# One stream of key tiles through a three-mixer attention kernel, with maxima and sums taken apart between two engines

## The chip, the cores and the metric

One core of a Trainium2 chip runs the whole program. The metric is device time in microseconds (us), and less is better. Five engines take part: TensorE (PE, with its weight loads shown as PEld), VectorE (DVE), ScalarE (ACT), GpSimd (POOL) and SyncE (SP, which issues the DMAs). Each works through its own instructions in order and waits on semaphores for the others.

## The reference

An input of 2048 rows by 1024 columns goes through one encoder layer in float32. After a modulated RMS norm, one projection feeds three groups of attention heads; their gated outputs are projected back, added to the input and normed.

```python
h = rmsnorm(x, norm_g) * (1.0 + scale) + shift
z = h @ w_in
a_out = mla_mixer(...)           # 6 heads, q and k of 64 + 32 rotary columns, mask by chunks of 64
b_out = chunk_band_mixer(...)    # 5 heads, own chunk + 8 chunks before, relative bias
c_out = forgetting_mixer(...)    # 5 heads, causal by frame, forget-gate bias in the logits
y = concat([a_out*silu(a_gate), b_out*silu(b_gate), c_out*silu(c_gate)]) @ w_out
out = rmsnorm(x + gate * y, final_g)
```

Each mixer is a softmax over the keys that its mask allows, times the values: `p = softmax(where(mask, s, -1e30)); o = p @ v`.

## The kernel before, in words

The rows are worked off in two halves of 1024. In each half, `stage_lv` makes the latent projections and the values, and `attention` then goes through 16 heads; each head has two blocks of 512 queries. At the end of half 1 comes the output projection (`out_units`), the last half of it after the attention.

Products that need float32 accuracy are split into a high and a low part of type fp32r, so a projection (`mm3_units`, L348 to L350) is three matmuls per 128 rows of contraction, and a score tile is two or three.

A block goes over its key tiles of 128 keys. One tile is `scores(n)`: the matmuls into a PSUM bank `st` (three banks; L994 and L1009 for kinds B and C, L1070, L1071 and L1074 for kind A), three exponentials on ACT (L744, L745, L747: the high part `ph`, a float32 copy `p32`, and one in place), the low part `pl` on DVE (L748), and the running sum `acc` on POOL (L753). Three tiles later `values(n)` multiplies by the values (L762, L763) into the one PSUM bank `pv`. After the last tile, `end()` does the three value products that are left, copies `pv` out on ACT (L775, L777) and adds its halves on POOL (L778).

A block needs the maximum of each query row before its first score. `max_units` forms score rows on PE into one of two PSUM banks `mx` (L968, L979, L1057), DVE reduces each (L971, L980, L1058), and the last unit, `fin`, ends the chain at once: DVE reduces once more (L985, L1062), and in `m_rows` negates (L704), rounds (L705) and subtracts for a low part (L706); PE transposes the 128x128 pad (L708); DVE spreads the result by a mask into rows 96 to 127 of the query tile (L709).

The denominators take three later steps (`tail`): `sums` transposes `acc` on PE (L787), DVE adds up (L788), inverts (L789) and splits (L793, L794); `rows` transposes the 128x32 pad (L800) and masks it into 512 columns (L801); `gate` multiplies by a matrix of ones (L808), so that every partition has every inverse, DVE multiplies by the gate path (L810), POOL by the values (L811), and a DMA stores.

What sets the order: `attention` calls one unit per tile, and after each unit calls shares of two lists: `fill` (projections and loads of the next head, output projection, next half's input) and maxima of the next block. The order in the source is a priority; a scheduler at build time moves instructions within it, and on the chip each engine keeps the resulting order.

```python
def step(n):
    scores(n)
    if n >= LAG:
        values(n - LAG)
```

Of the kernel before, what the change touches and what calls it, by code (L numbers as in the profile page):

```python
# [61 lines left out]
def kernel(ctx: ExitStack, tc: tile.TileContext, a: dict, out: bass.AP):  # L62
# [195 lines left out]
    mall = const.tile([128, 128], BF16, name="mall")  # L258
    V.memset(mall, -BIG)
# [3 lines left out]
    rpads = [const.tile([128, 32], F32R, name=f"rpad{i}") for i in range(2)]  # L263
    rrow = const.tile([128, 512], F32R, name="rrow")
    for t in mpads + rpads + [rrow]:
        G.memset(t.bitcast(F32), 0.0)
# [43 lines left out]
    def gate_row(pool):  # L310
# [11 lines left out]
        for c in range(2):  # L322
            p = pst("pj")
            T.matmul(p, lhsT=ones, rhs=acc[:, 512 * c:512 * c + 512], start=True, stop=True)
            V.tensor_tensor(bg[:, 512 * c:512 * c + 512], p[0:1, :], bg[:, 512 * c:512 * c + 512], op=ALU.add)
        dma(out=d_gate, in_=bg)
# [372 lines left out]
    def m_rows(pool, m4, dst, c8=None):  # L699

        mp = mpads[counters["m"] % 2]
        counters["m"] += 1
# [4 lines left out]
        tp = pst("mx")  # L707
        T.transpose(tp[:, 0:128], mp.bitcast(F32), ident)  # L708
        V.tensor_tensor(dst[96:128, :].rearrange("p (j t) -> p j t", j=4),  # L709
                        tp[96:128, None, 0:128].to_broadcast([32, 4, 128]),  # L710
                        mmask[96:128, :].rearrange("p (j t) -> p j t", j=4), op=ALU.mult)

    def body_units(pool, kind, tb, par, scale, qk, V_of, sg_of, dst):
# [12 lines left out]
        def scores(n):  # L726
# [13 lines left out]
            v0, v1 = c0, c1  # L740
            p32 = pool.tile([128, 512], F32, tag="acc" if n == 0 else "p32", name="p32", bufs=2 if n == 0 else 4)
            ph = pool.tile([128, 512], F32R, tag="ph", name="ph", bufs=PB)
            pl = pool.tile([128, 512], F32R, tag="pl", name="pl", bufs=PB)
# [4 lines left out]
            V.tensor_tensor(pl[:, v0:v1], st[:, v0:v1], ph[:, v0:v1].bitcast(F32), op=ALU.subtract)  # L748
            if n == 0:
                box["acc"] = p32  # L750
            else:
                acc = box["acc"]
                G.tensor_tensor(acc[:, v0:v1], acc[:, v0:v1], p32[:, v0:v1], op=ALU.add)  # L753
            box[n] = (ph, pl, c0, c1)

        def values(n):
# [3 lines left out]
            ph, pl, c0, c1 = box[n]  # L760
# [4 lines left out]
        def step(n):  # L765
            scores(n)
            if n >= LAG:
                values(n - LAG)

        def end():  # L770
            for n in range(max(len(js) - LAG, 0), len(js)):
                values(n)
# [5 lines left out]
            G.tensor_tensor(oa[o0:o1, :], oa[o0:o1, :], ob[o0:o1, :], op=ALU.add)  # L778
            box["oa"] = oa


        def sums():
# [6 lines left out]
            V.reciprocal(s4, s4)  # L789
            i = counters["r"] % 2  # L790
            counters["r"] += 1
            rp = rpads[i]
            V.tensor_scalar(rp[:, 0:4], s4, 0.5, 0.0, op0=ALU.mult, op1=ALU.add)  # L793
            V.scalar_tensor_tensor(rp[:, 4:8], in0=s4, scalar=0.5, in1=rp[:, 0:4].bitcast(F32), op0=ALU.mult, op1=ALU.subtract)  # L794
            box["rp"], box["rw"] = rp, rrow

        def rows():
            rp, rw = box["rp"], box["rw"]
            tp = pst("mx")
            T.transpose(tp[0:32, 0:128], rp.bitcast(F32), ident)  # L800
            V.tensor_tensor(rw[0:32, :].rearrange("p (j t) -> p j t", j=4),  # L801
                            tp[0:32, None, 0:128].to_broadcast([32, 4, 128]),
# [326 lines left out]
    def attention(heads, made, first, mids):  # L1129
# [24 lines left out]
        for _, u in tail:  # L1154
            u()
# [170 lines left out]
```

## Time and profile before

| what | value |
|---|---|
| three runs | 1902.49, 1903.47, 1904.70 us |
| median | 1903.47 us |
| the profiled execution | 1901.45 us |
| its span, first to last instruction | 1899.7 us |
| mean granted TensorE clock, as a share of full speed | 0.971 |
| busy share PE, DVE, ACT, POOL | 92%, 72%, 63%, 53% |

The span is what the profiler records; 1.75 us lie around it. Busy time is the time in which an engine has an instruction in execution. Matmuls overlap, so the start of one to the start of the next says more of PE's pace than the duration of one. An idle time in a group's row is what the engine stood still just before those instructions, and the name behind the arrow is the instruction that ended the wait.

### The profile page before, as it was taken

The numbers are of one execution on the slowest core, as the hardware profiler recorded it, in microseconds if no ns is written. First come the engines' busy times: TensorE is split into PE (matmuls) and PEld (weight loads), VectorE is DVE, ScalarE is ACT, GpSimd is POOL, SyncE is SP. The second block draws the span as 40 slices with busy tenths as digits, with TensorE's granted clock in tenths as the row PEclk, the third lists the DMA queues.
The fourth block names the chain that finished last, engine by engine and source line by source line (L and its number), as shares of the span: only waits on it lengthen the run. The fifth ranks groups of instructions, "written<-read, shape, count | busy, mean of one in ns | idle before, by whom it ended". The sixth has DMA issues, their size and how long they took to land.

```text
span 1899.7 us, 28618 instructions
## 1 busy us (share of the span) xinstructions
PE 1743.7 (92%) x8786; PEld 1416.1 (75%) x8786; DVE 1364.4 (72%) x3204; ACT 1191.9 (63%) x2550; POOL 1009.4 (53%) x943
## 2 busy tenths in 40 slices
PE   3999999898999987899999999999899989898997
PEld 3899877676777764899777787777677667776786
DVE  7764468887868789554567878888788888767543
ACT  2552356576767776342367778889888989554611
POOL 1320145666555656120155656767677878665744
PEclk9999999899999998899999999999999989999999
DMA  7534935334223332133943232222333344232243
GB/s 285 150 96 120 254 113 149 102 110 151 80 77 96 102 99 64 57 120 117 250 116 85 82 89 77 73 57 66 95 98 87 99 121 120 77 100 70 70 136 111
DMA packets 139997, 209.85 MB, mean 110 GB/s; under 512 B 18734, under 2 KB 72494, under 8 KB 139764
## 3 DMA queue, kind: packets, MB, share of 16 engines
q1 hardware_dynamic: 139844, 208.03, 36.7%
q8 instruction: 70, 1.15, 0.2%
q14 instruction: 83, 0.68, 0.1%
HBM read 154.05 MB, written 57.38 MB: 111 GB/s over the span
## 4 chain that ended last, share of the span: by engine, by line
PE 46%; DVE 8%; ACT 3%; issue 2%; POOL 2%; DMA 1%; SPq 0%; POOLq 0%; DVEq 0%; ACTq 0%
PE pj L348 6%; PE pj L350 6%; PE pj L349 6%; PE pv L762 3%; PE pv L763 3%; PE st L1009 2%; PE st L994 2%; PE mx L1057 2%; PE st L1074 2%; PE st L1070 2%; PE mx L968 1%; PE st L1071 1%; DVE pl L748 1%; PE st L348 1%; PE st L349 1%
## 5 line engine op out<-in xcount | busy, mean ns | idle before, releaser
L753 POOL TENSOR_TENSOR p<-p,p 128x512 f32<-128x512 f32 (+2 forms) x516 | 561.5, 1088 | 252.0 <-ACT p L745 194.3
L744 ACT ACTIVATE ph<-st 128x512 fp32r<-128x512 f32 (+1 forms) x580 | 323.1, 557 | 191.5 <-PE pv L762 99.8
L748 DVE TENSOR_TENSOR pl<-st,ph 128x512 fp32r<-128x512 f32 (+1 forms) x580 | 342.5, 593 | 92.8 <-ACT st L747 85.5
L747 ACT ACTIVATE st<-st 128x512 f32<-128x512 f32 (+1 forms) x580 | 330.5, 570 | 0.0
L745 ACT ACTIVATE p<-st 128x512 f32<-128x512 f32 (+1 forms) x580 | 322.9, 557 | 0.9 <-POOL p L753 0.9
L348 PE MATMUL pj<-hT,whi 128*128 128x512 f32 x544 | 223.8, 411 | 8.2 <-ACT q L925 8.2
L349 PE MATMUL pj<-hT,whi 128*128 128x512 f32 x544 | 220.1, 405 | 0.0
L350 PE MATMUL pj<-hT,wlo 128*128 128x512 f32 x544 | 219.5, 403 | 0.0
L763 PE MATMUL pv<-pl,v 128*128 128x512 f32 (+1 forms) x580 | 208.8, 364 | 5.3 <-DVE pl L748 5.3
L762 PE MATMUL pv<-ph,v 128*128 128x512 f32 (+1 forms) x580 | 211.6, 367 | 0.5 <-ACT ph L744 0.4
L1058 DVE TENSOR_REDUCE pm<-mx 128x1 f32<-128x512 f32 (+2 forms) x240 | 142.1, 603 | 18.5 <-PE mx L1057 16.1
L778 POOL TENSOR_TENSOR oa<-oa,ob 64x512 f32<-64x512 f32 x64 | 84.0, 1313 | 120.6 <-ACT ob L777 108.5
L971 DVE TENSOR_REDUCE pm<-mx 128x1 f32<-128x512 f32 (+2 forms) x200 | 118.8, 605 | 25.2 <-PE mx L970 12.5
L763 PEld LDWEIGHTS pv<-pl,v 128*128 128x128 f32 x580 | 110.5, 190 | 24.4 <-DVE pl L748 11.7
L762 PEld LDWEIGHTS pv<-ph,v 128*128 128x128 f32 x580 | 111.3, 192 | 18.9 <-ACT ph L744 5.4
L994 PE MATMUL st<-q,k 128*128 128x512 f32 (+1 forms) x340 | 122.6, 362 | 2.0 <-DVE pl L748 1.8
L348 PEld LDWEIGHTS pj<-hT,whi 128*128 128x128 f32 x544 | 105.8, 195 | 23.7 <-ACT q L925 9.1
L1009 PE MATMUL st<-q,k 128*128 128x512 f32 (+1 forms) x340 | 121.7, 379 | 0.2
L350 PEld LDWEIGHTS pj<-hT,wlo 128*128 128x128 f32 x544 | 104.8, 193 | 19.6
L349 PEld LDWEIGHTS pj<-hT,whi 128*128 128x128 f32 x544 | 105.6, 194 | 15.8
L1070 PE MATMUL st<-q,k 96*128 96x512 f32 x240 | 94.8, 395 | 9.3 <-DVE pl L748 8.4
L348 PE MATMUL pj<-wo,oh 128*128 128x512 f32 x256 | 102.2, 399 | 0.0
(408 smaller groups left out, 4349.0 us busy)
## 6 DMA issues: line engine op xcount, KB each, us to landing
wr<-in_w_in SPq DMA_DIRECT2D x54, 512.0 KB
wr<-in_x SPq DMA_DIRECT2D x34, 512.0 KB
v<-dva SPq DMA_DIRECT2D x36, 256.0 KB
q<-dqa SPq DMA_DIRECT2D x48, 192.0 KB
k<-dka SPq DMA_DIRECT2D x72, 128.0 KB
wa<-in_w_ada SPq DMA_DIRECT2D x16, 512.0 KB
do<-oo SPq DMA_DIRECT2D x64, 128.0 KB
wr<-do SPq DMA_DIRECT2D x128, 64.0 KB
```

The costliest lines, as they stand in the source:

```text
L348: T.matmul(dst, lhsT=lh, rhs=rh, start=i == 0, stop=False)
L349: T.matmul(dst, lhsT=lh, rhs=rl, start=False, stop=False)
L350: T.matmul(dst, lhsT=ll, rhs=rh, start=False, stop=i == n - 1)
L744: A.activation(ph[:, v0:v1], st[:, v0:v1], AF.Exp, scale=scale)
L745: A.activation(p32[:, v0:v1], st[:, v0:v1], AF.Exp, scale=scale)
L747: A.activation(st[:, v0:v1], st[:, v0:v1], AF.Exp, scale=scale)
L748: V.tensor_tensor(pl[:, v0:v1], st[:, v0:v1], ph[:, v0:v1].bitcast(F32), op=ALU.subtract)
L753: G.tensor_tensor(acc[:, v0:v1], acc[:, v0:v1], p32[:, v0:v1], op=ALU.add)
L762: T.matmul(pv[:, c0:c1], lhsT=vt, rhs=ph[:, c0:c1], start=n == 0, stop=False)
L763: T.matmul(pv[:, c0:c1], lhsT=vt, rhs=pl[:, c0:c1], start=False, stop=n == len(js) - 1)
L994: T.matmul(st[:, c0:c1], lhsT=k2[:, ks], rhs=q2[:, c0:c1], start=True, stop=False)
L1009: T.matmul(st[:, c0:c1], lhsT=k1[:, ks], rhs=q1[:, c0:c1], start=False, stop=True)
```

## The change

Five things are changed together.

1. **One stream of tiles.** A tile is now three calls: `scores` (matmuls and exponentials), `parts` (L762 of the changed file: `pl` on DVE, the sum on POOL) and `values`. `settle` runs ahead of the next tile's scores: the `parts` of the tile before and the `values` of the tile three back, whatever block or head that belongs to. `end` runs where the last values of a block are taken, two tiles into the next block.
2. **Maxima in three units.** `negate` (DVE), an empty unit, and `put` (PE transposition, DVE spread). The negation has one reduction that writes the negated maximum for kinds A and C; kind B has a reduction and one more operation with its bias. The low part of the maximum is left out, on both sides of the softmax alike.
3. **Sums.** The inverse is written to a float32 pad and no longer split before the transposition; ACT takes its high part (L805) and DVE the low part (L806) from 64 rows of 128 columns. Four matmuls of 128 columns with constant selecting matrices `sel` (L811) take the place of one of 512 columns. The gate path is multiplied in on POOL at `end`; its factor 0.5 goes into the row that is read in the output projection and the gate vector.
4. **Narrow tiles.** A score tile with 128 allowed columns is now 128 wide, not 256; the 79 matmuls that masked the other half (`no_tile`, L820) go, and the bias matmuls are cut to fit.
5. **Constants.** `mall`, the mask constant and a 512-column row pad go; `sel` is loaded through the ring `wr` of three buffers and rounded on DVE.

```diff
-    mmask = load_const("mmask", [128, 512])
+    sel = const.tile([128, 4, 128], F32R, name="sel")
+    raw = wr()
+    dma(out=raw[:, 0:512], in_=a["sel"])
+    V.tensor_copy(sel.rearrange("p j t -> p (j t)"), raw[:, 0:512])
...
-        t4 = pool.tile([128, 4], F32, tag="t4", name="t4")
-        V.tensor_scalar(t4, m4, -1.0, 0.0 if c8 is None else c8, op0=ALU.mult, op1=ALU.add)
-        V.tensor_copy(mp[:, 96:100], t4)
-        V.tensor_tensor(mp[:, 100:104], t4, mp[:, 96:100].bitcast(F32), op=ALU.subtract)
...
+        def negate():
+            mp = box["mp"] = mpads[counters["m"] % 2]
+            counters["m"] += 1
+            if c8 is None:
+                V.tensor_reduce(mp[:, 96:100], pm_of(), axis=AX.X, op=ALU.max, negate=True)
+            else:
+                m4 = pool.tile([128, 4], F32, tag="m4", name="m4")
+                V.reduce_max(m4, pm_of(), axis=AX.X)
+                V.tensor_scalar(mp[:, 96:100], m4, -1.0, c8(), op0=ALU.mult, op1=ALU.add)
+
+        def put():
+            tp = pst("mx")
+            T.transpose(tp[:, 0:128], box["mp"].bitcast(F32), ident)
+            V.tensor_tensor(dst()[96:128, :].rearrange("p (j t) -> p j t", j=4),
...
+        return [negate, lambda: None, put]
...
+            G.tensor_tensor(oa[o0:o1, :], oa[o0:o1, :], sg_of()[o0:o1, :], op=ALU.mult)
...
-            V.reciprocal(s4, s4)
...
-            V.tensor_scalar(rp[:, 0:4], s4, 0.5, 0.0, op0=ALU.mult, op1=ALU.add)
-            V.scalar_tensor_tensor(rp[:, 4:8], in0=s4, scalar=0.5, in1=rp[:, 0:4].bitcast(F32), op0=ALU.mult, op1=ALU.subtract)
...
+            V.reciprocal(rp[:, 0:4], s4)
...
+            T.transpose(tp[:, 0:128], box["rp"], ident)
+            A.activation(rw[0:64, :], tp[0:64, 0:128], AF.Copy)
+            V.tensor_tensor(rw[64:128, :], tp[0:64, 0:128], rw[0:64, :].bitcast(F32), op=ALU.subtract)
...
-            T.matmul(rb, lhsT=ones_r, rhs=box["rw"], start=True, stop=True)
+            for t in range(4):
+                T.matmul(rb[:, 128 * t:128 * t + 128], lhsT=sel[:, t, :], rhs=box["rw"], start=True, stop=True)
...
-            V.tensor_tensor(oo[o0:o1, :], rb[o0:o1, :], sg_of()[o0:o1, :], op=ALU.mult)
-            G.tensor_tensor(oo[o0:o1, :], oo[o0:o1, :], oa[o0:o1, :], op=ALU.mult)
+            V.tensor_tensor(oo[o0:o1, :], rb[o0:o1, :], box["oa"][o0:o1, :], op=ALU.mult)
...
-            if v1 - v0 < 256:
-                c0, c1 = (256, 512) if v0 else (0, 256)
...
-                if d == 3:
-                    no_tile(st, 2)
...
+        def settle():
+
+            if part:
+                part.pop()()
+            if len(behind) == LAG or behind and not todo[0]:
+                values, end, t = behind.pop(0)
+                values()
+                if end:
+                    end()
+                    tail.extend((clock[0] + d, u) for d, u in zip((1, 3, 5), t))
+
+        def step(scores, share, maxima):
+            settle()
+            if scores:
+                scores[0]()
+                part.append(scores[1])
+                behind.append(scores[2:])
+                todo[0] -= 1
+            while tail and tail[0][0] <= clock[0]:
+                tail.pop(0)[1]()
+            for spread, upto in zip((fill,) + maxima, share):
+                spread.upto(upto)
+            clock[0] += 1
```

How the instructions move is seen on two engines, at the passage from the first to the second block of one head of kind C in half 1. On DVE before, from the last reductions of the maxima to the last step of the sums (`m` is the row maximum, `t` its negative, `s` the row sums):

```order
L985 TENSOR_REDUCE m_14510<-pm 128x4
L922 TENSOR_TENSOR q_14551<-pj,q_14550 64x512
L704 TENSOR_SCALAR t_14512<-m_14510 128x4
L923 TENSOR_TENSOR k_14549<-pj,k_14549 64x512
L705 CAST mpad_252<-t_14512 128x4
L706 TENSOR_TENSOR mpad_252<-t_14512,mpad_252 128x4
L709 TENSOR_TENSOR q_14256<-mx,c_mmask 32x512
L788 TENSOR_REDUCE s_14613<-mx 128x4
L789 RECIPROCAL s_14613<-s_14613 128x4
L793 TENSOR_SCALAR rpad_253<-s_14613 128x4
L794 SCALAR_TENSOR_TENSOR rpad_253<-s_14613,rpad_253 128x4
L801 TENSOR_TENSOR rrow<-mx,c_mmask 32x512
```

The same place of the changed kernel:

```order
L712 TENSOR_REDUCE mpad_252<-pm 128x4
L762 TENSOR_TENSOR pl<-st,ph 128x256
L917 TENSOR_TENSOR q_14336<-pj,q_14335 64x512
L721 TENSOR_TENSOR q_14045<-mx,sel 32x512
L918 TENSOR_TENSOR k_14334<-pj,k_14334 64x512
L762 TENSOR_TENSOR pl<-st,ph 128x128
L796 TENSOR_REDUCE s_14428<-mx 128x4
L799 RECIPROCAL rpad_253<-s_14428 128x4
```

L704, L705 and L706 have no counterpart, nor have L793 and L794: the negation is in the reduction itself (L712), and the inverse is written to the pad directly (L799). The spread of the sums (L801) has become L806, which stands behind seven instructions of other tiles.

On PE before, at the same passage (`L763 ... 128x256` are the last value products of the first block, `q_14256` and `q_14257` the queries of the second):

```order
L763 MATMUL pv<-pl,v 128x256
L994 MATMUL st<-q_14257,k_13752 128x512
L349 MATMUL pj<-hT,whi 128x512
L350 MATMUL pj<-hT,wlo 128x512
L348 MATMUL pj<-hT,whi 128x512
L349 MATMUL pj<-hT,whi 128x512
L350 MATMUL pj<-hT,wlo 128x512
L348 MATMUL pj<-hT,whi 128x512
L708 MATMUL mx<-c_ident,mpad_252 128x128
L787 MATMUL mx<-c_ident,p_14273 128x128 x4
L349 MATMUL pj<-hT,whi 128x512
L350 MATMUL pj<-hT,wlo 128x512
```

And in the changed kernel:

```order
L776 MATMUL pv<-ph,v 128x384
L353 MATMUL pj<-hT,whi 128x512
L720 MATMUL mx<-c_ident,mpad_252 128x128
L777 MATMUL pv<-pl,v 128x384
L986 MATMUL st<-q_14046,k_13538 128x512
L776 MATMUL pv<-ph,v 128x256
L777 MATMUL pv<-pl,v 128x256
L986 MATMUL st<-q_14046,k_13538 128x512
L776 MATMUL pv<-ph,v 128x128
L354 MATMUL pj<-hT,wlo 128x512
L795 MATMUL mx<-c_ident,p_14067 128x128 x2
```

The transposition of the maxima (L708, now L720) stands ahead of the last value products, not behind all of them, and the value products of the first block alternate with the scores of the second.

## Rows read from the trace of the kernel before

**Rows 1.** The page: busy us, share of the span, instructions of three engines

```profile
PE 1743.7 (92%) x8786; PEld 1416.1 (75%) x8786; DVE 1364.4 (72%) x3204; ACT 1191.9 (63%) x2550; POOL 1009.4 (53%) x943
```

**Rows 2.** Windows by stage: length, busy us and count per engine, clock, DMA share, GB/s

```profile
250.00:755.00 505.00, 463.36 (x2297) 356.84 (x2295) 409.91 (x946) 356.55 (x785) 296.17 (x276) 0.97 0.34 101
955.00:1500.00 545.00, 528.31 (x2567) 411.17 (x2566) 442.15 (x946) 442.35 (x952) 369.98 (x326) 0.99 0.28 81
1500.00:1620.00 120.00, 107.44 (x462) 81.36 (x461) 105.90 (x186) 106.02 (x218) 99.14 (x77) 0.93 0.44 128
```

**Rows 3.** Groups by line, PE: busy us, mean ns; idle us before, releasers

```profile
L708 PE MATMUL mx<-c_ident,mpad 128*128 128x128 f32 x64 | 20.9, 326 | 35.7 <-DVE mpad L706 34.6 <-DVE xrt L154 0.4
...
L800 PE MATMUL mx<-c_ident,rpad 128*32 128x128 f32 x64 | 18.0, 281 | 11.0 <-DVE rpad L794 10.1 <-DVE pm L980 0.7
...
L787 PE MATMUL mx<-c_ident,p 128*128 128x128 f32 x256 | 41.8, 286 | 9.5 <-DVE pm L1058 6.2 <-POOL p L753 3.3
...
L1057 PE MATMUL mx<-k,q 128*128 128x512 f32 (+2 forms) x240 | 87.5, 386 | 12.2 <-DVE pm L1058 11.4 <-DVE s L788 0.7
L1070 PE MATMUL st<-q,k 96*128 96x512 f32 x240 | 94.8, 395 | 9.3 <-DVE pl L748 8.4 <-DVE xrt L154 0.4
```

**Rows 4.** Groups by line, DVE: the small operations of maxima and sums

```profile
L704 DVE TENSOR_SCALAR t<-m 128x4 f32<-128x4 f32 x44 | 20.4, 464 | 0.9
L704 DVE TENSOR_SCALAR t<-m,c 128x4 f32<-128x4 f32 x20 | 7.5, 376 | 0.6
L705 DVE CAST mpad<-t 128x4 fp32r<-128x4 f32 x64 | 18.5, 288 | 1.7
L706 DVE TENSOR_TENSOR mpad<-t,mpad 128x4 fp32r<-128x4 f32 x64 | 15.6, 243 | 1.8
L1062 DVE TENSOR_REDUCE m<-pm 128x4 f32<-128x4 f32 (+3 forms) x24 | 3.7, 155 | 0.1
L793 DVE TENSOR_SCALAR rpad<-s 128x4 fp32r<-128x4 f32 x64 | 23.2, 363 | 0.9
L794 DVE SCALAR_TENSOR_TENSOR rpad<-s,rpad 128x4 fp32r<-128x4 f32 x64 | 18.7, 292 | 1.0
```

**Rows 5.** Timeline 1252.5 to 1257: start us, us, engine, line, operation, idle before

```profile
1252.96 1.26 POOL L778 TENSOR_TENSOR oa<-oa,ob 64x512 f32<-64x512 f32 x1 [1.81 <-ACT ob L777]
...
1253.33 3.22 DVE L704 TENSOR_SCALAR t<-m 128x4 f32<-128x4 f32 x1
...
1254.18 2.33 POOL L339 TENSOR_TENSOR wlo<-wr,whi 128x1024 fp32r<-128x1024 f32 x1
...
1257.00 0.48 PE L708 MATMUL mx<-c_ident,mpad 128*128 128x128 f32 x1 [3.73 <-DVE mpad L706]
```

**Rows 6.** Windows around the first and last of four waits, columns as in Rows 2

```profile
345.00:357.00 12.00, 8.08 (x30) 6.76 (x31) 9.69 (x13) 4.93 (x13) 5.86 (x6) 0.72 0.64 213
...
1538.00:1554.00 16.00, 9.35 (x28) 6.21 (x28) 14.94 (x21) 11.18 (x21) 10.61 (x7) 0.68 0.50 152
```

**Rows 7.** Waits in total: engine and line, releaser, us, times, longest us

```profile
ACT ph L744 <- PE pv L762: 99.8, 61, 8.8
...
ACT oa L775 <- PE pv L763: 74.7, 46, 3.6
```

**Rows 8.** Groups by line and shape, PE: prices for the products that change

```profile
L808 PE MATMUL mx<-rrow,ones_r 128*128 128x512 f32 x64 | 28.3, 442 | 1.6 <-DMA wr<-do 0.8 <-DVE rrow L801 0.8
...
L820 PE MATMUL st<-mall,ident_b 128*128 128x128 bf16 x79 | 17.9, 227 | 0.0
```

**Rows 9.** Source view of L775: ns min/median/max, first and last start

```profile
L775 ACT ACTIVATE oa<-pv x64: 579/592/597, 265.9 to 1799.0; 64x512 f32<-64x512 f32 x64
```

**Rows 10.** Timeline of the start, 26 to 41 us, columns as in Rows 5

```profile
26.26 12.83 SPq L337 DMA_DIRECT2D wr<-in_w_in  x3
35.70 0.75 DVE L193 TENSOR_SCALAR xn<-wr,xrr 128x1024 f32<-128x1024 f32 x1
...
39.74 1.05 ACT L338 ACTIVATE wbhi<-wr 128x1024 fp32r<-128x1024 f32 x1
```

More of the change, by code (lines that the diff above doesn't have):

```diff
@@ L747, in scores, with parts @@
             A.activation(st[:, v0:v1], st[:, v0:v1], AF.Exp, scale=scale)
-            V.tensor_tensor(pl[:, v0:v1], st[:, v0:v1], ph[:, v0:v1].bitcast(F32), op=ALU.subtract)
+            box[n] = (st, p32, ph, c0, c1)
+        def parts(n):
+            st, p32, ph, c0, c1 = box[n]
+            pl = pool.tile([128, 512], F32R, tag="pl", name="pl", bufs=PB)
+            V.tensor_tensor(pl[:, c0:c1], st[:, c0:c1], ph[:, c0:c1].bitcast(F32), op=ALU.subtract)
             if n == 0:
@@ L981, in piece @@
                                        op0=ALU.add, op1=ALU.max, accum_out=pm[:, q, c:c + 1])
-            def fin():
-                m4 = pool.tile([128, 4], F32, tag="m4", name="m4")
-                V.reduce_max(m4, box["pm"][:, :, 0:nch], axis=AX.X)
-                m_rows(pool, m4, self.qb[b][0], self.c8)
-            return [lambda q=q, c=c: piece(q, c) for q in range(4) for c in range(nch)] + [fin]
+            return [lambda q=q, c=c: piece(q, c) for q in range(4) for c in range(nch)] + m_rows(
+                pool, box, lambda: box["pm"][:, :, 0:nch], lambda: self.qb[b][0], (lambda: self.c8) if kind == "B" else None)
         def qk(self, b, st, j, c0, c1):
@@ L1132, in attention, with tiles_of @@
         Spread(heads[0].max_units(heads[0].blocks[0])).upto(1)
-        tail, clock = [], [0]
+        tail, clock, behind, part = [], [0], [], []
+        def settle():
[19 more added lines that the diff above has]
+            clock[0] += 1
+        def tiles_of(body):
+            units, end, t = body
+            return [(*u[:2], u[2], end if n == len(units) - 1 else None, t) for n, u in enumerate(units)]
+        todo = [10 ** 6]
         for n, head in enumerate(heads):
@@ L1139, in attention @@
             m2 = Spread(nxt.max_units(nxt.blocks[0])) if nxt else Spread([])
-            (u0, t0), (u1, t1) = head.body(b0), head.body(b1)
+            u0, u1 = tiles_of(head.body(b0)), tiles_of(head.body(b1))
             n0, n1 = len(u0), len(u1)
-            def steps(us, off, maxima, share):
-                for i, u in enumerate(us):
-                    u()
-                    while tail and tail[0][0] <= clock[0]:
-                        tail.pop(0)[1]()
-                    fill.upto(((off + i + 1) / (n0 + n1)) ** 0.8)
-                    maxima.upto(share(i))
-                    clock[0] += 1
-            steps(u0, 0, m1, lambda i: (i + 1) / (n0 - 2))
-            tail += [(clock[0] + d, u) for d, u in zip((2, 4, 6), t0)]
-            steps(u1, n0, m2, lambda i: (i + 1 - 0.4 * n1) / (0.6 * n1 - 1) if i + 1 < n1 else 1)
-            tail += [(clock[0] + d, u) for d, u in zip((2, 4, 6), t1)]
-        for _, u in tail:
-            u()
+            if not nxt:
+                todo[0] = n0 + n1
+            for i, u in enumerate(u0):
+                step(u, (((i + 1) / (n0 + n1)) ** 0.8, (i + 1) / (n0 - 1)), (m1,))
+            for i, u in enumerate(u1):
+                step(u, (((n0 + i + 1) / (n0 + n1)) ** 0.8, (i + 1 - 0.4 * n1) / (0.6 * n1 - 1) if i + 1 < n1 else 1), (m2,))
+        while behind or tail:
+            step(None, (), ())
     hT = hT0
@@ L1243, in _constants @@
     m = np.zeros((128, 512), np.float32)
-    for i in range(8):
-        for base in (0, 96):
-            m[base + i, 128 * (i % 4):128 * (i % 4) + 128] = 1.0
-    c["mmask"] = m
+    for t in range(4):
+        for base in (0, 64, 96):
+            m[base + t, 128 * t:128 * t + 128] = 1.0
+    c["sel"] = m
     c["inv_freq"] = (10000.0 ** (-np.arange(0, 32, 2) / 32)).astype(np.float32)[None, :]
```

72 lines of the change are left out of this document (19 added, 53 removed).

## The prediction

> **What bounds the kernel now.** I read the page first: PE is busy 92% of the span, DVE 72%, ACT 63%, POOL 53% [rows 1]. The windows by stage say the same more finely: 463 of 505 us in the attention of half 0, 528 of 545 in most of half 1, and 107 of 120 between 1500 and 1620, where DVE and ACT are both at 106 [rows 2]. So PE sets the end, in its own order, and time can come from two places only: PE's work, or the gaps in which PE waits for an engine that is itself not full. The groups of PE with idle time ahead show where those gaps are. The largest is the transposition of the maxima: 35.7 us, 34.6 of them ended by DVE's L706. The transposition of the inverses has 11.0, that of the sums 9.5, the maxima products L1057 12.2, the scores L1070 9.3 [rows 3].
>
> Why is DVE late there, at 72%? Its groups answer. The chain of a maximum has three operations on four columns behind the last reduction, and their means are 0.464, 0.288 and 0.243 us, where the reduction of the same size takes 0.155 [rows 4]. The timeline shows one case: L704 lasts 3.22 us while POOL works on L778 and then L339, and PE stands 3.73 us before L708 [rows 5]. The sums have two such operations, 0.363 and 0.292 [rows 4]. [...]
>
> Last, the windows around such waits: the granted clock falls to 0.72 and 0.68 in the first and last of four that I looked at [rows 6]; the two in between read 0.72 as well. [...]
>
> **The change, term by term**, against the profiled execution of 1901.45 us (span 1899.7); the median of the runs is 2.0 us above it.
>
> *Maxima.* DVE loses 20.4 + 18.5 + 15.6 = 54.5 us of busy time [rows 4]; kind B keeps its 7.5. In 44 blocks the chain behind the last reduction falls from 0.155 + 0.464 + 0.288 + 0.243 = 1.15 us to one reduction of 0.155, and that is of the kind that is never stretched. Between negation and transposition an empty unit is put, so that the two mostly fall into different steps. Against that, the transposition now stands closer to the last maximum product, as the order on PE shows, and in half 0, where a block has four steps, both units fall into one. Of the 35.7 us [rows 3] between a bit over a quarter and all should go, -10 to -35.7. I take three quarters, -27, since the long single waits are those with a stretched operation.
>
> *Sums.* L793 and L794 go, 23.2 + 18.7 = 41.9 us of DVE [rows 4]; the masked spread of 512 columns becomes 128 columns on ACT and on DVE, both off PE's path while the third step is two steps later. PE's waits of 11.0 and 9.5 [rows 3]: -2 to -20.5, taken -9, mostly the first, because the second is ended by other reductions.
>
> *Clock.* Four windows lose 3 x 12 x 0.28 + 16 x 0.32 = 15.2 us of full-speed time [rows 6]. Part of it is idle anyway. 0 to -15, taken -10.
>
> *The stream.* ACT stood 99.8 us before its first exponential and 74.7 us before the copies of `pv`, both for value products [rows 7]: before, the exponentials of tile n wait for a buffer that `values` of tile n-3 frees, and that stood behind the scores of n on PE; now it stands ahead. ACT is not the bound, so this pays only where PE then waits for ACT and DVE in turn: the 9.3 us of L1070 and 12.2 of L1057 [rows 3]. 0 to -21.5, taken -12. What is moved with it: `parts` goes behind a step's reductions on DVE, and POOL's two adds and multiplications per block stay two, at the same size, one now earlier. DMAs per block stay one store, and SP is passed by nothing.
>
> *PE's own work.* Four products of 128 columns cost what four transpositions do, 41.8 / 64 = 0.65 us; the one of 512 costs 28.3 / 64 = 0.44 [rows 3, 8]: 64 x 0.21 = +13.4. The transposed pad grows from 32 to 128 columns: 20.9 against 18.0 us for 64 [rows 3], +2.9. The 79 masking products go: 0 to -17.9 [rows 8]; they start close behind their neighbours, so -4.5. Narrow tiles: some 360 products (two or three for scores, two for values, in 79 tiles) lose 128 columns, worth between 0 (if the weight load sets the pace) and (442 - 286) / 3 = 52 ns, the difference of rows with 512 and 128 columns [rows 3, 8]: 0 to -18.9, taken -4, near the low end, since four products of 128 columns already cost more than one of 512. Together +8, from -21 to +16.
>
> [...] PE's weight loads are busy 1416.1 us for 8786, 0.161 us each [rows 1], and I count them as covered by the products beside them. [...]
>
> *Start.* `sel` takes the third buffer of `wr`, in which the first weights landed from 26.26 us on; they now wait until 36.45, when L193 has freed a buffer, and ACT first reads them at 39.74 [rows 10]. 0 to +3, taken +1.5.
>
> Sum: -27 - 9 - 10 - 12 + 8 + 1.5 = -48.5, so 1901.45 - 48.5 = 1853, and 1855 for the median.
>
> **Rivals.**
> *The wait stays where it is.* The transposition stands closer to the last maximum product, DVE has a `pl` in its queue that waits for ACT, and PE waits as before. Then maxima -10, sums -4, clock 0, stream -6, the rest +9.5: -10.5, so 1893. For it: ACT and DVE are both full between 1500 and 1620 [rows 2]. Against: the stretched operations are plainly the long waits [rows 5].
>
> *Slower: the one `pv` bank.* Before, three steps lay between the copies of `pv` and the first value product of the next block; now it is one. Where ACT is behind with its exponentials, PE stands until both copies are through, 2 x 0.592 = 1.18 us [rows 9], at 62 passages: +73, so 1855 + 73 = 1928. It decides if the copies end later than PE's work of one step. For it: ACT at 88% between 1500 and 1620. Against: in 46 of 64 blocks ACT was there first and waited for PE, 74.7 us in all [rows 7].
>
> *All of it.* Maxima -33, sums -18, clock -15, stream -21, PE's work 0, start +1.5: -85.5, so 1818. It needs PE to find every operand ready; the 88% on DVE and ACT in the late stage speak against it.
>
> *The change does little that counts*: DVE was never the bound, the gaps close up elsewhere and PE's 16 us eat the rest, within 3.8 us of 1903.
>
> **How the numbers follow.** A difference of 0.2%, 3.8 us, is about what a measurement of this kernel can tell from none. My case, 1825 to 1885, has 0.58; the wait that stays 0.16; all of it 0.12; no difference 0.04; slower by the bank 0.10. The range from 1820 to 1898 leaves out the bank, no difference, and part of the largest gain. Faster: 0.58 + 0.12 + most of 0.16 = 0.85; same 0.05; slower 0.10.
>
> **What would show it.** In the profile after: the idle before the transposition of the maxima (now L720) near 9 us; small operations of DVE that are never longer than 0.2 us in kinds A and C; no window around a maximum with a clock near 0.7; the idle of ACT before its first exponential and before the copies under 60 us together; four selecting products near 0.65 us. DVE should fall by some 130 us to about 1235: 54.5 + 41.9, some 25 of the spread and some 10 of narrow tiles. Wrong it would be with an idle of PE before the first value product (L776) in the tens of us, or with L720 waiting as long as L708 did.

## The result, and the profile after

| what | before | changed |
|---|---|---|
| executions, median | 1904.09 us (4) | 1884.97 us (4, from 1880.27 to 1887.48) |
| the profiled execution, its span | 1901.45, 1899.7 us | 1887.48, 1885.4 us |
| mean granted clock | 0.971 | 0.979 |

The ratio is 0.9895, with an interval from 0.9872 to 0.9919. The change is faster by 1.05%, 19 us. The forecast was 49 us, with a range from 1820 to 1898: the sign and the range held, the size did not. One execution of the run e5_copy_dve below, 1965.12 us at a clock of 0.838, was in a slower state and is left out of its median. The page of the changed kernel, to be read beside [rows 1]:

```profile
PE 1743.9 (92%) x8899; PEld 1429.7 (76%) x8899; DVE 1254.3 (67%) x2905; ACT 1181.6 (63%) x2614; POOL 985.7 (52%) x902
```

PE is busy for the same 1744 us, so the 14.3 us by which the span is shorter are idle time of PE: 1899.7 - 1743.7 = 156.0 before, 141.5 now. Where it went, and where it came up again, stands in PE's groups by line. Of the kernel before, four rows that were not shown yet:

```profile
L762 PE MATMUL pv<-ph,v 128*128 128x512 f32 (+1 forms) x580 | 211.6, 367 | 0.5 <-ACT ph L744 0.4
L763 PE MATMUL pv<-pl,v 128*128 128x512 f32 (+1 forms) x580 | 208.8, 364 | 5.3 <-DVE pl L748 5.3
...
L968 PE MATMUL mx<-k,q 96*128 96x512 f32 (+2 forms) x200 | 73.9, 384 | 0.5 <-ACT k L924 0.2
L979 PE MATMUL mx<-k,q 96*128 96x384 f32 (+3 forms) x140 | 45.3, 346 | 1.0 <-ACT k L924 0.6
```

And the same view of the changed kernel:

```profile
L776 PE MATMUL pv<-ph,v 128*128 128x512 f32 (+1 forms) x580 | 215.1, 371 | 11.9 <-ACT ob L784 10.6 <-ACT ph L753 0.5
L777 PE MATMUL pv<-pl,v 128*128 128x512 f32 (+1 forms) x580 | 213.0, 368 | 12.0 <-DVE pl L762 11.4
...
L1054 PE MATMUL st<-q,k 96*128 96x512 f32 x240 | 92.4, 385 | 1.8 <-DVE pl L762 1.1
...
L1044 PE MATMUL mx<-k,q 128*128 128x512 f32 (+2 forms) x240 | 89.8, 394 | 20.6 <-DVE pm L1045 17.3 <-DVE oo L813 2.5 <-DVE xvv L176 0.4
...
L963 PE MATMUL mx<-k,q 96*128 96x512 f32 (+2 forms) x200 | 73.0, 388 | 2.9 <-ACT k L919 1.1 <-DVE pm L966 0.8 <-DVE oo L813 0.3
L974 PE MATMUL mx<-k,q 96*128 96x384 f32 (+3 forms) x140 | 45.8, 353 | 6.9 <-ACT k L919 3.3 <-DVE s L796 2.6 <-DVE pm L975 0.5
L811 PE MATMUL mx<-rrow,sel 128*128 128x128 f32 x256 | 40.6, 275 | 4.8 <-DVE rrow L806 3.7 <-DVE pm L1045 1.1
L795 PE MATMUL mx<-c_ident,p 128*128 128x128 f32 x256 | 40.5, 276 | 0.0
...
L720 PE MATMUL mx<-c_ident,mpad 128*128 128x128 f32 x64 | 18.7, 293 | 7.3 <-DVE mpad L716 5.2 <-DVE mpad L712 1.9
...
L804 PE MATMUL mx<-c_ident,rpad 128*128 128x128 f32 x64 | 17.7, 276 | 3.6 <-DVE rpad L799 2.1 <-DVE pm L1045 1.4
```

Beside [rows 3] this is a ledger. Gone: 28.4 us ahead of the transposition of the maxima (35.7 to 7.3), 9.5 and 7.4 ahead of the two of the sums, 7.5 ahead of the scores (L1070, now L1054); 52.8 in all. Come: the value products from 5.8 to 23.9, the maxima products of all kinds from 13.7 to 30.4, the product of the gate from 1.6 to 4.8; 38.0 in all. The waits that the forecast wanted gone are gone, and seven tenths of their sum stands ahead of other products.

ACT's idle, which the stream was to remove, moved as well. Before, it was for value products [rows 7] and in part for scores (the waits in total):

```profile
ACT ph L744 <- PE st L1009: 49.2, 46, 7.0
...
ACT ph L744 <- PE st L1074: 38.6, 30, 5.2
```

Now it is for scores:

```profile
ACT ph L753 <- PE st L996: 137.5, 110, 6.5
...
ACT ph L753 <- PE st L1056: 109.0, 72, 6.8
...
ACT oa L782 <- PE pv L777: 19.4, 8, 7.5
```

With the two lines of [rows 7], ACT waited 262.3 us for PE at these places before, and it waits 265.9 now: the sum is hardly changed.

On DVE, L712 is as short as forecast, and the sums' spread too (the groups by line):

```profile
L806 DVE TENSOR_TENSOR rrow<-mx,rrow 64x128 fp32r<-64x128 f32 x64 | 18.2, 284 | 3.5 <-ACT rrow L805 1.6
...
L716 DVE TENSOR_SCALAR mpad<-m,c 128x4 fp32r<-128x4 f32 x20 | 7.9, 393 | 0.6
...
L712 DVE TENSOR_REDUCE mpad<-pm 128x4 fp32r<-128x4 f32 (+3 forms) x44 | 6.9, 156 | 0.5
```

But the longest waits of the maxima products are still made as [rows 5] shows, by operations that the change does not touch. DVE's timeline, and then PE's, from 1624.5 on:

```profile
1624.71 2.24 DVE L156 TENSOR_TENSOR xrr<-xry,xrt 128x1 f32<-128x1 f32 x1
1626.99 2.38 DVE L1106 SCALAR_TENSOR_TENSOR wr<-wr,xrr,row 128x512 f32<-128x512 f32 x2
1629.40 0.69 DVE L1045 TENSOR_REDUCE pm<-mx 128x1 f32<-128x512 f32 x1
```

```profile
1625.33 0.39 PE L1044 MATMUL mx<-k,q 128*128 128x512 f32 x1
1630.15 0.79 PE L1044 MATMUL mx<-k,q 128*128 128x512 f32 x1 [4.43 <-DVE pm L1045]
```

An operation on one column takes 2.24 us (POOL is in L1081 at that time), two operations of 2.38 us together and a reduction of the maxima stand behind it, and PE waits 4.43 us for the bank `mx` that the reduction frees. Around it, and around a like wait of 3.17 us that ends near 473, the granted clock is at 0.76 (windows, columns as in [rows 2]):

```profile
466.00:480.00 14.00, 10.44 (x38) 8.18 (x37) 9.15 (x23) 6.46 (x13) 4.82 (x5) 0.76 0.45 125
1622.00:1636.00 14.00, 9.57 (x32) 7.51 (x31) 11.35 (x16) 5.22 (x11) 6.44 (x5) 0.76 0.34 110
```

So windows at a low clock remain, but the clock is higher on the whole: the span times what its mean clock lacks is 1899.7 x 0.029 = 55.1 us before and 1885.4 x 0.021 = 39.6 now, part of it in time in which PE stands idle anyway.

### The profile page after: what moved, and what is told of

Same layout as the page of the kernel before. It is cut to its first block, busy times and chain, and to the rows that moved or that the text cites. A ratio compares the mean times of both kernels' runs of the same rounds, so it can differ in the third digit from the quotient of the medians.

```text
span 1885.4 us, 28584 instructions
## 1 busy us (share of the span) xinstructions
PE 1743.9 (92%) x8899; PEld 1429.7 (76%) x8899; DVE 1254.3 (67%) x2905; ACT 1181.6 (63%) x2614; POOL 985.7 (52%) x902
## 4 chain that ended last, share of the span: by engine, by line
PE 36%; DVE 5%; ACT 5%; issue 3%; POOL 1%; DMA 1%; DVEq 0%; POOLq 0%; ACTq 0%
PE pj L352 5%; PE pj L354 5%; PE pj L353 5%; PE pv L777 3%; PE pv L776 3%; PE st L996 2%; PE st L986 2%; PE mx L1044 2%; PE st L1054 2%; PE st L1055 1%; PE mx L963 1%; PE st L1056 1%; ACT st L756 1%; ACT p L754 1%; DVE pl L762 1%
## 5 line engine op out<-in xcount | busy, mean ns | idle before, releaser
L767 POOL TENSOR_TENSOR p<-p,p 128x512 f32<-128x512 f32 (+3 forms) x516 | 547.5, 1061 | 301.0 <-ACT p L754 267.3
L753 ACT ACTIVATE ph<-st 128x512 fp32r<-128x512 f32 (+1 forms) x580 | 297.7, 513 | 265.4 <-PE st L996 137.5
L762 DVE TENSOR_TENSOR pl<-st,ph 128x512 fp32r<-128x512 f32 (+1 forms) x580 | 333.3, 577 | 175.1 <-ACT st L756 161.2
L756 ACT ACTIVATE st<-st 128x512 f32<-128x512 f32 (+1 forms) x580 | 302.8, 522 | 0.0
L754 ACT ACTIVATE p<-st 128x512 f32<-128x512 f32 (+1 forms) x580 | 296.6, 511 | 0.0
L776 PE MATMUL pv<-ph,v 128*128 128x512 f32 (+1 forms) x580 | 215.1, 371 | 11.9 <-ACT ob L784 10.6
L777 PE MATMUL pv<-pl,v 128*128 128x512 f32 (+1 forms) x580 | 213.0, 368 | 12.0 <-DVE pl L762 11.4
L1045 DVE TENSOR_REDUCE pm<-mx 128x1 f32<-128x512 f32 (+2 forms) x240 | 139.5, 603 | 22.6 <-PE mx L1044 20.6
L776 PEld LDWEIGHTS pv<-ph,v 128*128 128x128 f32 x580 | 111.6, 192 | 40.4 <-ACT ob L784 23.1
L777 PEld LDWEIGHTS pv<-pl,v 128*128 128x128 f32 x580 | 111.2, 192 | 38.9 <-DVE pl L762 22.0
L966 DVE TENSOR_REDUCE pm<-mx 128x1 f32<-128x512 f32 (+2 forms) x200 | 116.6, 605 | 30.6 <-PE mx L963 17.1
L352 PEld LDWEIGHTS pj<-hT,whi 128*128 128x128 f32 x544 | 105.0, 193 | 23.8 <-ACT q L920 10.1
L1044 PE MATMUL mx<-k,q 128*128 128x512 f32 (+2 forms) x240 | 89.8, 394 | 20.6 <-DVE pm L1045 17.3
L354 PE MATMUL pj<-wo,ol 128*128 128x512 f32 x256 | 102.6, 401 | 2.1 <-POOL ol L1081 2.1
```

The source lines that it names most:

```text
L352: T.matmul(dst, lhsT=lh, rhs=rh, start=i == 0, stop=False)
L354: T.matmul(dst, lhsT=ll, rhs=rh, start=False, stop=i == n - 1)
L753: A.activation(ph[:, v0:v1], st[:, v0:v1], AF.Exp, scale=scale)
L754: A.activation(p32[:, v0:v1], st[:, v0:v1], AF.Exp, scale=scale)
L756: A.activation(st[:, v0:v1], st[:, v0:v1], AF.Exp, scale=scale)
L762: V.tensor_tensor(pl[:, c0:c1], st[:, c0:c1], ph[:, c0:c1].bitcast(F32), op=ALU.subtract)
```

## The experiments

The medians of before, measured along with the runs, lie between 1902.4 and 1906.4 us, so a step from one run to another is good to some 3 or 4 us; where it is smaller, the ratio to before with its interval stands beside it.

| run | what it is | median, us | ratio to before, interval |
|---|---|---|---|
| e1_maxima | before + maxima | 1874.81 | 0.9851 (0.9836 to 0.9865) |
| e2_stream | before + stream | 1903.60 | 1.0002 (0.9988 to 1.0016) |
| e3_nostream | changed, old step loop | 1878.14 | 0.9870 (0.9855 to 0.9885) |
| e4_scores_first | changed, scores ahead of settling | 1890.95 | 0.9940 (0.9925 to 0.9955) |
| e5_copy_dve | changed, second copy on DVE | 1879.98 | 0.9889 (0.9853 to 0.9924) |
| e6_parts_now | changed, parts in their own step | 1887.14 | 0.9903 (0.9888 to 0.9918) |
| e7_one_unit | before + maxima, one unit | 1858.78 | 0.9758 (0.9740 to 0.9776) |
| e8_max_sums | e1 + sums | 1877.62 | 0.9854 (0.9835 to 0.9872) |
| e9_max_narrow | e1 + narrow tiles | 1864.22 | 0.9780 (0.9765 to 0.9796) |
| e10_one_narrow | e7 + narrow tiles | 1866.32 | 0.9804 (0.9790 to 0.9819) |
| e11_empty_ahead | e7, two empty units ahead | 1874.78 | 0.9849 (0.9830 to 0.9869) |
| e12_after_one | changed, maxima in one unit | 1889.24 | 0.9931 (0.9915 to 0.9947) |
| e13_nostream_one | e3, maxima in one unit | 1882.56 | 0.9886 (0.9864 to 0.9907) |
| e14_sums_chain | e9 + short chain of the sums | 1854.54 | 0.9733 (0.9718 to 0.9747) |
| e15_drain | changed, drained at each block's end | 1886.79 | 0.9900 (0.9885 to 0.9915) |
| e17_before_empty | before, two empty units | 1914.45 | 1.0051 (1.0034 to 1.0068) |
| e18_four | e14, four products for one | 1873.14 | 0.9841 (0.9817 to 0.9864) |
| e19_chain_stream | e14 + stream | 1862.14 | 0.9782 (0.9759 to 0.9806) |

### The parts apart

e1_maxima takes over `m_rows` and the lists of `max_units` as changed (with the old mask), and nothing else:

```diff
+        return [negate, lambda: None, put]
```

> The kernel before with the maxima of the change alone (one negating reduction, an empty unit, the transposition as a unit of its own, no low part). Theory S (the stream is what failed; the maxima gave what was forecast): PE's idle before the transposition falls from 35.7 to some 8 us and the slow clock goes with it, so 25 to 40 us faster than before, 1864 to 1879. Rival M (waits move: the pace is set by the round of PE, ACT and DVE, and a wait removed comes up again at the next tile): the idle before the transposition falls as much, that before the products of maxima, values and scores grows by most of it, 5 to 12 us faster, 1892 to 1899.

Measured: 29 us faster, ten more than the whole change. The idle ahead of the transposition falls from 35.7 to 12.1 us (8 expected), and 1873.8 x 0.023 = 43.1 us are lost to the clock, 12 fewer than before. Theory S has this one.

e2_stream puts `scores`, `parts`, `values`, `settle` and the new loop into the kernel before:

```diff
-            (u0, t0), (u1, t1) = head.body(b0), head.body(b1)
+            u0, u1 = tiles_of(head.body(b0)), tiles_of(head.body(b1))
```

> The kernel before with the one stream of tiles alone (parts and values of earlier tiles settled ahead of a tile's scores, end two tiles into the next block). Theory S: PE waits for the copies of pv (some 10 us before the value products) and for pl (some 7 us more), and the products of the maxima wait longer: 10 to 40 us slower than before, 1914 to 1944. Rival M: the stream moves waits about as well, within 8 us of before. The forecast's own term would be 12 us faster, 1892.

Measured: no difference. Theory S expected a loss here and the forecast a gain, so M has this one. Its waits say why:

```profile
ACT ph L743 <- PE st L1072: 131.5, 80, 6.8
ACT ph L743 <- PE st L1007: 113.4, 91, 7.0
...
ACT oa L773 <- PE pv L768: 29.7, 23, 4.3
```

ACT no longer waits for value products to start its exponentials. It waits for scores, which on PE now stand behind value products: 274.6 us in these three rows, where the four rows of before make 262.3.

e3_nostream is the changed kernel with the loop of before:

```diff
+        def step(n):
+            scores(n)
+            parts(n)
+            if n >= LAG:
+                values(n - LAG)
```

> The changed kernel with the step loop of before (scores, parts and values of tile n-3 in one step, the last three values and the copies at a block's end), all else as changed. Theory S: without the stream's waits the other terms stand, -27 - 9 - 10 to -20 + 8 + 1.5: 1850 to 1870, faster than the changed kernel by 15 to 35. Rival M: within 6 us of the changed kernel, 1879 to 1891.

Measured: 1878.1, between the two expectations, 7 us ahead of the changed kernel. The stream costs something there; but it is not all, since e1 with fewer changes is faster still. So the sums or the narrow tiles had to cost too. e8_max_sums and e9_max_narrow add the one or the other to e1; of e9 the core is

```diff
-            if v1 - v0 < 256:
-                c0, c1 = (256, 512) if v0 else (0, 256)
```

and e8 is e3 with these two lines, `no_tile` and the old bias products put back.

> Maxima and sums of the changed kernel, old step loop, old widths of tiles with the masking products. By the forecast's terms the sums give 9 us of waits and cost 16.3 of PE (four selecting products, wider pad) and 1.5 at the start: 8.8 us slower than the maxima alone, 1880 to 1887. If the sums' waits are worth what their idle says (15.1 + 7.2 us in the run with the maxima alone): about as fast as the maxima alone, 1871 to 1878.

> Maxima of the changed kernel and the narrow tiles (128 wide, no masking products, bias products cut), old sums and old step loop. By the forecast's terms 8.5 us faster than the maxima alone, 1863 to 1869. If PE's pace at 128 columns is that of 256 and the masking products were hidden: 1872 to 1878.

Measured: the sums +2.8 us on e1, which is inside the second expectation and too small to be told from none by the ratios, and the narrow tiles -10.6, as forecast. On top of the narrow tiles the sums cost more: e3 stands 13.9 us behind e9.

### Sums: the chain and the products

e14_sums_chain keeps the old spread and the one product, and shortens the chain alone:

```diff
-            V.reciprocal(s4, s4)
...
-            V.tensor_scalar(rp[:, 0:4], s4, 0.5, 0.0, op0=ALU.mult, op1=ALU.add)
-            V.scalar_tensor_tensor(rp[:, 4:8], in0=s4, scalar=0.5, in1=rp[:, 0:4].bitcast(F32), op0=ALU.mult, op1=ALU.subtract)
...
+            V.reciprocal(rp[:, 0:4], s4)
```

> Maxima and narrow tiles (1864.2 us) and of the sums only the short chain: the inverse goes straight to the pad and its low part is left out; the spread by the mask, the one product of 512 columns and the gate's order stay as before. PE waited 11.8 us before the transposition of the inverses. If the four selecting products and the wider pad are what made the sums cost 14 us (their own work is 16): 1852 to 1862. If a wait removed comes up elsewhere: 1862 to 1870.

Measured: 9.7 us faster than e9, 1854.54, the fastest of all kernels here. The wait went and did not come back: the transposition of the inverses has 0.3 us of idle ahead, where e9 has 11.8. e18_four then cuts its product:

```diff
-            T.matmul(rb, lhsT=ones_r, rhs=box["rw"], start=True, stop=True)
+            for t in range(4):
+                T.matmul(rb[:, 128 * t:128 * t + 128], lhsT=ones_r, rhs=box["rw"][:, 128 * t:128 * t + 128], start=True, stop=True)
```

> The version with maxima, narrow tiles and the short chain of the sums (1854.5 us), its one product of 512 columns by the matrix of ones cut into four of 128 columns with the same weights: the four selecting products' price alone. By the forecast's rows (0.65 us for four transpositions of 128 columns, 0.44 for one product of 512) 64 x 0.21 = 13.4 us slower, 1864 to 1872. If they lie beside waits that PE has anyway: 1850 to 1860.

Measured: 18.6 us slower, a us above the first expectation. The first line of the pages, of e14 and then of e18:

```profile
PE 1719.5 (93%) x8707; PEld 1407.8 (76%) x8707; DVE 1275.8 (69%) x2904; ACT 1165.9 (63%) x2550; POOL 984.3 (53%) x903
```

```profile
PE 1739.0 (93%) x8899; PEld 1431.4 (76%) x8899; DVE 1270.5 (68%) x2904; ACT 1166.9 (62%) x2550; POOL 984.3 (53%) x903
```

PE is busy 19.5 us longer, its idle time is the same (1852.5 - 1719.5 = 133.0, 1871.8 - 1739.0 = 132.8). Here is the price in pure form: 18.6 / 64 = 0.29 us for a block. The 5.0 us from e18 to e3 are left for the wider pad, the split on ACT and DVE, the gate's order and `sel` together, which were not tried one by one.

### The stream

Four edits of the changed kernel each take away one thing that its stream could pay with.

```diff
 # e4_scores_first, in step
+            if scores:
+                scores[0]()
             settle()
 # e5_copy_dve, in end
-            A.activation(ob[o0:o1, :], pv[o0:o1, :], AF.Copy)
+            V.tensor_copy(ob[o0:o1, :], pv[o0:o1, :])
 # e6_parts_now, in step
-                part.append(scores[1])
+                scores[1]()
 # e15_drain, behind each of the two loops over tiles
+            drain()
```

> The changed kernel with a tile's scores put ahead of the settling of earlier tiles; the rest of the stream stays. Theory S, if it is the order within a step that costs: the first value products of a block have a tile's scores more of time before them, their wait for the copies (10.6 us) and for pl (11.4) goes for the most part, 10 to 20 us faster than the changed kernel, 1865 to 1875. If it is the stream's passage between blocks that costs, or by rival M: within 6 us of the changed kernel.

> The changed kernel with the second of the two copies of pv at a block's end on DVE instead of ACT, so that both can run side by side. Theory B (the one pv bank is what the stream pays with): PE's wait before the value products for the copies (10.6 us) falls below 4 and the time by 4 to 10 us, 1875 to 1881. Rival D (the round of PE, ACT and DVE sets the pace, PE would wait a little later anyway, and DVE gets 64 more operations of 0.6 us): within 4 us of the changed kernel, 1881 to 1889.

> The changed kernel with a tile's parts (pl, the sum) right behind its own scores, not a step later; values and end as changed. In the changed kernel PE waits 12.0 us before value products for pl and 30.4 before maxima products for their reductions. Theory Q (what the stream costs is that pl comes late and the reductions stand among late pl): these fall by a third or more, 1872 to 1880. Theory B (it is the passage over the one pv bank): they stay, 1882 to 1890.

> The changed kernel with the stream drained at each block's end: the last parts, the three values that are left and the copies come in a step of their own, as before; within a block the order is the stream's. Theory B (the passage between blocks over the one pv bank): PE's wait before the value products for the copies (10.6 us) goes and 5 to 10 us with it, 1875 to 1880. Theory Q (the order within a step): 1883 to 1892.

Measured: 1890.95, 1879.98, 1887.14, 1886.79. Three of them stay behind e3 by 8 us and more. e5 cannot be told by its interval from the changed kernel, nor from e3; its profile, of its slowest execution here (1898.53 us), still has 12.0 us of PE's wait for the copies, so the edit did not do what it was to do. In e6 the waits stay as they were (12.4 us ahead of L777, 33.0 ahead of maxima products). In e4 the idle ahead of L777 falls from 12.0 to 1.1 us and comes up elsewhere: ahead of the scores (3.9 to 14.0), for the copies (10.6 to 13.2) and ahead of the maxima products (30.4 to 33.2). Most is to be learnt from e15:

```profile
L776 PE MATMUL pv<-ph,v 128*128 128x512 f32 (+1 forms) x580 | 213.0, 371 | 3.3 <-ACT ob L784 2.4 <-ACT ph L753 0.7 <-DMA k<-dkpe 0.2
L777 PE MATMUL pv<-pl,v 128*128 128x512 f32 (+1 forms) x580 | 211.8, 375 | 24.1 <-DVE pl L762 23.0 <-DMA q<-d_eq_b 0.3
```

The wait for the copies falls from 10.6 to 2.4 us, as expected, and the wait of the very next product for `pl` rises from 11.4 to 23.0. Theory B falls, since its wait is there but has no price of its own; what Q names, the late `pl`, falls with e6. That the cost lies in the order within a block is left, and e4 shows one other order that is no better. e19_chain_stream puts the stream on the fastest version, with the edit of e2:

> The same version (1854.5 us) with the one stream of tiles put on: no selecting products, no copy of the rows on ACT. If the stream costs what it cost in the changed kernel (7 us), since PE's wait only moves from scores to values and maxima products: 1857 to 1866. If it cost that only together with the selecting products: 1845 to 1856.

Measured: 7.6 us slower than e14. Two more runs of the table, with the maxima in one unit, differ in the stream alone: e12 is 6.7 us slower than e13. So the stream costs some 7 us with and without the selecting products (by the ratios to before 4.8, 8.6 and 9.3 us, of which the first is within the noise), and nothing in the kernel before, where its own gain ahead of the old chain (the idle before L708 is 23.0 us in e2, where it was 35.7) may be what stands against it. Where the cost arises is read from e3, which differs from the changed kernel in the loop alone:

```profile
L776 PE MATMUL pv<-ph,v 128*128 128x512 f32 (+1 forms) x580 | 210.9, 366 | 1.0 <-ACT ph L753 1.0
L777 PE MATMUL pv<-pl,v 128*128 128x512 f32 (+1 forms) x580 | 207.0, 366 | 10.4 <-DVE pl L762 10.4
...
L1062 PE MATMUL st<-q,k 96*128 96x512 f32 x240 | 94.9, 395 | 14.5 <-DVE pl L762 13.9 <-DVE xrt L154 0.4
...
L1052 PE MATMUL mx<-k,q 128*128 128x512 f32 (+2 forms) x240 | 88.6, 390 | 14.4 <-DVE pm L1053 13.2 <-DVE s L804 0.5
```

With the stream PE's idle ahead of all scores falls from 19.0 to 3.9 us, and rises ahead of the value products from 11.4 to 23.9 and ahead of the maxima products from 19.3 to 30.4. From e14 to e19 it is 16.6 to 3.0, 8.0 to 29.3, and 24.0 to 23.3. PE's idle time as a whole grows by 4.0 us in the first pair and by 8.8 in the second. Which order would make the stream pay stays open.

### The list of a block's maxima

Negation and transposition in one unit, in e1 (e7), in the changed kernel (e12) and in e3 (e13); e10 is e7 with the narrow tiles:

```diff
-        return [negate, lambda: None, put]
+        return [lambda: (negate(), put())]
```

> The maxima of the changed kernel in the kernel before, but negation and transposition together in one unit as before, without the empty one: the chain is short, the separation is gone. If it is the short chain (one reduction that is never stretched in place of four operations): within 4 us of the maxima alone (1874.8), with an idle before the transposition of 10 to 18 us. If it is the separation into steps: 1885 to 1900, with 20 to 30 us of idle there.

> The kernel before with the short chain of the maxima in one unit and the narrow tiles; sums and step loop as before. The two parts have given 45 and 10.6 us in runs of their own. If they add: 1845 to 1852. If they pay with the same waits of PE: 1853 to 1861.

> The changed kernel with negation and transposition in one unit, no empty one; stream, sums, narrow tiles as changed. If the separation costs in the stream what it cost in the old step loop (16 us): 1865 to 1873. If the stream needs it (the negation then stands directly ahead of a waiting PE): 1880 to 1895.

> The changed kernel with the old step loop and with negation and transposition in one unit: short chain, sums and narrow tiles. If the separation's 16 us and the stream's 7 both come back: 1858 to 1866. Beside the run with the short chain and the narrow tiles alone it gives what the sums cost or bring: by the forecast's terms +9, by the two runs so far +3 to +14.

In e11 two empty units stand ahead of that one; in e17 the same two stand in the kernel before:

```diff
+        return [lambda: None, lambda: None, lambda: (negate(), put())]
```

> The maxima alone with the short chain, two empty units and then negation and transposition in one unit: the list of a block's maxima is as long as with the separation (so the maxima products are packed into as few steps), but nothing is apart. Theory K (what the separation costs is the packing of the products ahead of it): as slow as the separated one, 1868 to 1880. Theory L (it is the transposition put apart that costs, its hold on a bank of mx and its place on PE): as fast as the one unit, 1855 to 1864.

> The kernel before with two empty units ahead of the last unit of each block's maxima, nothing else: the maxima products are packed into fewer steps. If the packing costs whatever stands around it, as it did with the short chain (16 us): 1914 to 1924. If that was this schedule's own: within 6 us of before.

Measured: e7 is 16 us faster than e1, better than either expectation, with 7.0 us of idle ahead of the transposition; e11 is as slow as e1. So in that pair the transposition's place has no price: the list has three units behind the products instead of one, its shares are the same, and the products are packed into fewer steps. Theory K has it, and in the kernel before the same packing costs 8 to 10 us, with 10.1 us more of idle ahead of L708. But beside other parts the gain is gone: one unit is slower by 2.1 us with narrow tiles (e10 against e9), by 4.4 in e3 (e13, where 1858 to 1866 was expected) and by 4.3 in the changed kernel (e12), each hardly more than the noise. That the gains of e7 and of the narrow tiles add was refuted: 1866.3, where 1845 to 1852 was expected; on e7 the narrow tiles cost 7.5 us, where on e1 they gave 10.6. Each edit makes the scheduler lay the whole order anew, and the runs do not say which meeting of instructions decides.

## Why the prediction was wrong

From before to the changed kernel by runs, each step with the term of the forecast:

| step | runs | forecast, us | measured, us |
|---|---|---|---|
| maxima, with the clock | before, e1 | -27 - 10 | -28.9 |
| narrow tiles, no masking products | e1, e9 | -4 - 4.5 | -10.6 |
| short chain of the sums | e9, e14 | -9 | -9.7 |
| four selecting products | e14, e18 | +13.4 | +18.6 |
| wider pad, start, the rest of the sums | e18, e3 | +2.9 + 1.5 | +5.0 |
| one stream | e3, changed | -12 | +6.8 |
| sum | | -48.7 | -18.8 |

Of the 30 us that are missing on this path, 19 are the stream's, 8 the maxima's and the clock's, 5 the products'; the narrow tiles gave 2 more. By the ratios to before the measured steps are -28.4, -13.5, -8.9, +20.6, +5.5 and +4.8. The steps depend on the path: over e7, e10, e13 and e12 they are -45.0 for the maxima in one unit, +7.5 for the narrow tiles, +16.2 for the sums (+8.8 by the forecast's terms), +6.7 for the stream and -4.3 for the units apart. The stream misses its term by 19 us on both paths, the sums by 5 to 7. The maxima and the narrow tiles miss to one side on the one and to the other side on the other, so their shares are open.

**The stream** is the step that failed in kind: 12 us faster by the forecast, 7 us slower in e3 against the changed kernel, and no gain in any of four places. The text said that ACT's waits pay "only where PE then waits for ACT and DVE in turn", took the idle of L1070 and L1057 for that, and gave 12 of their 21.5 us. The scores' idle did go (9.3 to 1.8). But value products now stand ahead of the scores, and wait themselves: for the copies and for `pl`, 18 us more. The tile's round over PE, ACT and DVE became no shorter, as ACT's 262.3 and 265.9 us of waiting for PE show; another product meets its end. The text took ACT's 99.8 us as the wait to be removed and left out the 87.8 for scores that stood beside it. The bound "0 to -21.5" should have had a loss at its other end.

**The pv bank**, as a rival, had its mechanism right and its price wrong: PE waits there for ACT's copies, but 10.6 us in all and not 73, and e15 shows that taking them away gains nothing. The check that was announced, an idle of tens of us before L776, came out at 11.9.

**Maxima and clock.** The size of the wait was right (-28.4 of idle, -27 forecast), and so was the reason: L712 has a mean of 156 ns, and never more than 170, where four operations stood; the reductions of that size in the kernel before, L985 and L1062, last at most 167 and 170 ns, where L704 goes up to 3219 and L705 to 3519. The forecast also held the empty unit to be a help; beside the old sums and tile widths it costs 16 us (e1 and e11 against e7), and in the changed kernel nothing that can be told from the noise. The clock, read from one execution of each, gave back 12 us in e1 and 15.5 in the changed kernel, beside the 10 forecast, and yet e1 falls 8 short of the two terms' sum: its own wait falls by 23.6, not 27, and maxima products, scores and the inverses' transposition wait 3.7, 5.2 and 4.1 us longer in it than before. In the changed kernel the two windows at 0.76 show one way in which that comes about: a stretched operation that remains (L156, 2.24 and 1.94 us there, where its rows have a median of 0.160) stalls another product, which waits 4.43 and 3.17 us, and the clock is low there. The clock's term was also taken from the lowest windows: the four at 0.72 and 0.68 were read together with two more, at 0.83 and 0.79, which the text left out.

**The sums' chain** was right within a us (e14 against e9), but not as a part of the whole, where 16.3 us of PE's work were known to stand against it. Of these, the 2.9 us for the wider pad do not show in its row: 17.7 us for L804 with 128 columns, 18.0 for L800 with 32.

**The products.** I took their price from the durations of rows, 0.65 against 0.44 us, which gives 0.21; measured alone it is 0.29. That is 18.6 us for 64 times four against one, and the forecast's 13.4 were too little by 5.2. The forecast counted the weight loads as covered by the products beside them; as an estimate, 192 added loads at the 0.161 us that one took before would be 30.9 us for this edit alone, too much by 12.3.

The announced checks: ahead of L720 7.3 us (9 forecast), yes; four selecting products 40.6 / 64 = 0.63 us (0.65), yes; DVE down by 110 us, not 130; ACT's idle before its first exponential and the copies under 60 us, plainly no, 265.4 before the exponentials alone, since it moved to the scores; no window near 0.7 around a maximum, where the two shown read 0.76.

## What to carry to other kernels

An engine that waits less for one thing need not wait less on the whole, as ACT's 262.3 and 265.9 us show here: ask what the freed wait meets next, on each engine of the round, before it is put into a sum. A short chain on a small operation paid in both places where it was tried alone (maxima in e7, 45.0 us; sums in e14, 9.7), and splitting one product of 512 columns into four did not (e18, 18.6 us slower); a change that mixes such parts is worth taking apart, since two of its parts and half of a third (e14) give 49 us where the whole gives 19. Where a scheduler lays the order anew, prices of single edits do not add, here by up to 18 us (e10), and each combination has to be measured.

## What the runs showed of the hardware

- In the changed kernel a DVE operation on a single column (L156, `xrr`) took 2.24 us beside a POOL operation of 2.37; the 24 of its row have a median of 0.160. The 44 reductions L712, on the same engine and as small, lie between 0.144 and 0.170 us. The remaining negations L716 take from 0.229 to 0.778 us, and the four longest, of 0.72 us and more, each run beside a POOL operation (L767). The operation on the single column ends with POOL's L1081 (1624.58 + 2.37 and 1624.71 + 2.24 us are both 1626.95). Why it lasts so long there was not shown.
- Four products of 128 columns with one and the same weight tile cost 0.29 us more than one of 512 (e18 against e14), and the weight loads' busy time rose by 23.6 us for 192 more (0.123 each): each of the four has a load of its own, though the weights are the same (256 loads in L811 of e18, 64 in L810 of e14).
